# Row sums of the softmax shared by two rows, later turns on TensorE, six probability buffers, and one spread for two maxima, in a hybrid attention layer on one Trainium2 core

## The chip, the cores and the metric

The program runs on one core of one Trainium2 chip. The metric is the device time of one execution in microseconds (us). Three executions of the kernel before took 1028.60, 1028.52 and 1027.94 us, with a median of 1028.52 us. The engines are called as in the profile: PE is TensorE, DVE is VectorE, ACT is ScalarE, POOL is GpSimd, and SP is the engine that issues most of the DMAs.

## What is computed

One encoder layer over 1024 tokens of width 1024. A normed input goes through one projection into the queries, keys and values of two token mixers. Group A is attention in a sliding window with a learned sink logit for each of its 8 heads; group B is neighbourhood attention on a 16 x 64 grid with 8 heads. Their outputs are normed, joined and projected, and a gated feed-forward part follows. The change touches the softmax of both mixers, and the scales of the output projection. Cut to that:

```python
# group A, per block of 128 queries and 384 keys (256 at the ends)
s = einsum('bqgrd,bkgd->bgrqk', q_i, k_i) * scale
s = where(valid, s, -1e30)
m = maximum(max(s, axis=-1), sink_gr)
p = exp(s - m[..., None])
denom = sum(p, axis=-1) + exp(sink_gr - m)
o = einsum('bgrqk,bkgd->bgrqd', p, v_i) / denom
...
# group B
p = softmax(s + bias)
o = einsum('bhcij,bicjhd->bchd', p, v_win)
...
h = h + einsum('bse,ed->bsd', concat([rmsnorm(o_a), rmsnorm(o_b)]), w_out)
```

## The kernel before

All matrix products are made to single-precision accuracy from two halves, a high and a low part: three matmuls for each block of weights. PE runs its instructions in the order in which the program is written. The other engines are ordered by a scheduler, which moves instructions about within their dependences and priorities; each engine then works through its own list strictly in that order.

The attention stage lies between about 60 us and 345 us of the span. It is cut into *units*. Group A has 16 units (2 key heads x 8 blocks of queries), each with four *rows* (one row is one head and one block: 128 queries against 384 or 256 keys). Group B has 32 units, four for each of 8 heads, each with two rows. A unit's work on PE is a list of *events*: a score step for a row (`q_step`, two matmuls at L436), a value step (`v_step`, L525 in group A, L601 in group B) and, for some rows, a *turn* (four lines from L495, the matmuls at L498). Score steps run two to three units ahead of the value steps that use their rows. Between two events `fill` puts in blocks of the projections that are still owed (L172 to L174, three matmuls each), and later of the output projection (L180), by the rates in `RATES`. So PE has something to do nearly always.

A row passes through `softmax` (L458 to L492). On DVE, L466 adds the mask or bias to the scores, writes them to a buffer `p` and finds the row's extreme. On ACT, L470 takes the exponential and sums it into `sm`. On DVE, L471 takes the reciprocal of `sm`, one instruction for each row. Then the row leaves by one of four paths:

- T: POOL scales the row (L474); later PE turns it over by three transposes into a bank `pt` (L498), ACT copies the high part (L501) and DVE the low part (L502).
- D: DVE makes `by`, the reciprocal times a constant (L484); ACT writes the high part to a staging tile (L485), DVE the low part (L487), and a transposing DMA, here called a *flip*, carries both to the tile `turned` (L492, issued by SP).
- P: POOL scales the row (L474), ACT and POOL make the two parts (L480, L481), and a flip follows.
- Q: as D, but the low part is made on POOL by two instructions, a scaled copy `y` (L490) and a subtraction (L491).

Group A's rows go D, P, T, T (`PATH_A`); group B's go Q, Q, T, Q, Q, Q, T, Q for the eight blocks of a head (`PATH_B`). Two rows next to each other share one tile `turned` (the class `Rows`), of which three are in rotation, with a few spare ones. The buffers `p` are five in rotation (`PS`), `y` has one (`YS`); staging tiles are three. In group A, POOL first copies the sink logit into the buffer (L465).

Where turns stand among a unit's events is set by hand: `T_NEXT = (3, 8)` puts the two turns of the next unit at places 3 and 8 of this unit's events while group A is worked on, `T_B` does so in group B, and `T_AT` holds for the first unit.

`out_scales` (L891 to L903) runs once, at about 190 us. It needs the largest value of a vector of gains and of the rows' sums of the output weights, on all partitions; `top` makes each by a reduction on DVE, one transpose on PE (L255), and a second reduction on DVE (L256).

## Time and profile before

| | us |
|---|---|
| median of three executions | 1028.52 |
| the profiled execution, its own time | 1028.71 |
| the span of that execution, first to last instruction | 1026.6 |
| PE busy, of the span | 1009.0 (98%) |
| DVE busy | 875.2 (85%) |
| ACT busy | 675.8 (66%) |
| POOL busy | 214.6 (21%) |

The profiled execution's time is 2.1 us above its span, and 0.2 us above the median. The granted clock of PE is 0.997 of full speed. Matmuls overlap, so what PE's busy time shows is not how close to its peak it is; what it does show are the stretches in which PE stood still, and the view of waits says for whom. A number in brackets behind a row of a timeline is the time that the engine sat idle before that instruction, and who released it.

### The profile page before, as it was taken

The page shows a single profiled execution, that of the slowest core. Times are in us where ns is not written, and L with a number is a line of the kernel's source. Part 1 is how long each engine was busy: PE and PEld are TensorE (multiplying, and loading weights), DVE is VectorE, ACT ScalarE, POOL GpSimd, SP SyncE. Part 2 cuts the span into 40 slices and gives each one's busy share as a digit, 9 for nine tenths or more (in the row PEclk, how much of TensorE's full clock was granted, in tenths as well). Part 3 has the DMA queues.
Part 4 walks back from the last instruction along what each step waited for, and adds up shares of the span by engine and source line. Part 5 has one row for each costly group of instructions (what it writes and reads, how often), then busy time and mean ns, then how long its engine had stood idle before and what let it go on. Part 6 is the DMA issues. An engine that isn't in the chain of part 4 may idle for free.

```text
span 1026.6 us, 15663 instructions
## 1 busy us (share of the span) xinstructions
PE 1009.0 (98%) x5102; PEld 577.2 (56%) x5102; DVE 875.2 (85%) x1715; ACT 675.8 (66%) x1242; POOL 214.6 (21%) x339
## 2 busy tenths in 40 slices
PE   8999999999999999999999999999999999999996
PEld 6877777777775555544444444444444444444446
DVE  6799997767898799999897989888888879999865
ACT  7667787768687687645777777844544656655551
POOL 2225545777976210001000000000000000000002
PEclk9999999999999999999999999999999999999998
DMA  8566564786799874201787777723232778978734
GB/s 318 194 134 134 111 141 102 154 160 134 141 190 226 287 254 165 82 1 42 258 279 248 262 242 250 246 99 128 87 122 89 256 250 306 309 242 269 257 141 164
DMA packets 143938, 191.79 MB, mean 187 GB/s; under 512 B 77360, under 2 KB 88112, under 8 KB 143856
## 3 DMA queue, kind: packets, MB, share of 16 engines
q1 hardware_dynamic: 133264, 164.84, 56.2%
q10 hardware_dynamic: 10592, 25.95, 6.6%
q8 instruction: 40, 0.66, 0.3%
q14 instruction: 42, 0.34, 0.1%
HBM read 132.81 MB, written 28.57 MB: 157 GB/s over the span
## 4 chain that ended last, share of the span: by engine, by line
PE 75%; DVE 3%; DMA 2%; ACT 1%; issue 0%; POOL 0%; DVEq 0%; ACTq 0%; POOLq 0%
PE pj L180 7%; PE dn L1199 6%; PE dn L1198 6%; PE dn L1197 6%; PE z L1197 5%; PE z L1198 5%; PE z L1199 5%; PE x L1197 4%; PE y L1197 4%; PE x L1198 4%; PE y L1198 4%; PE y L1199 4%; PE x L1199 4%; PE pj L172 3%; PE pj L174 2%; PE pj L173 2%
## 5 line engine op out<-in xcount | busy, mean ns | idle before, releaser
L1199 PEld LDWEIGHTS <-wlo 128*128 128x128 f16 x898 | 87.9, 98 | 101.3
L1197 PEld LDWEIGHTS <-whi 128*128 128x128 f16 x898 | 88.1, 98 | 100.3
L1198 PEld LDWEIGHTS <-whi 128*128 128x128 f16 x898 | 87.9, 98 | 100.2
L1199 PE MATMUL dn<-xd,wlo 128*128 128x512 f16 (+1 forms) x330 | 120.4, 365 | 0.0
L1198 PE MATMUL dn<-xd,whi 128*128 128x512 f16 (+1 forms) x330 | 120.4, 365 | 0.0
L1197 PE MATMUL dn<-xd,whi 128*128 128x512 f16 (+1 forms) x330 | 120.4, 365 | 0.0
L172 PE MATMUL pj<-xgh,whi 128*128 128x512 f32 x248 | 106.8, 431 | 0.0
L1197 PE MATMUL z<-hg,whi 128*128 128x512 f16 x264 | 100.1, 379 | 0.0
L1198 PE MATMUL z<-hg,whi 128*128 128x512 f16 x264 | 100.1, 379 | 0.0
L1199 PE MATMUL z<-hg,wlo 128*128 128x512 f16 x264 | 100.1, 379 | 0.0
L470 ACT ACTIVATE p<-p,nm 128x385 f32<-128x385 f32 (+3 forms) x128 | 74.8, 584 | 35.7 <-DVE nm L466 27.1
L174 PE MATMUL pj<-xgh,wlo 128*128 128x512 f32 x248 | 97.7, 394 | 0.0
L173 PE MATMUL pj<-xgl,whi 128*128 128x512 f32 x248 | 97.4, 393 | 0.0
L1171 ACT ACTIVATE whi<-ws,m 128x512 f16<-128x512 f32 (+1 forms) x96 | 65.9, 708 | 35.6 <-DVE ws L1338 20.4
L1172 DVE SCALAR_TENSOR_TENSOR wlo<-ws,m,whi 128x512 f16<-128x512 f32 (+1 forms) x96 | 70.2, 741 | 17.9 <-ACT whi L1171 17.7
L1052 POOL TENSOR_TENSOR back<-back,cst 128x4 f32<-128x4 f32 (+1 forms) x7 | 2.8, 394 | 356.7 <-DVE back L1051 356.7
L1186 ACT ACTIVATE scan<-scan 128x1024 f32<-128x1024 f32 (+1 forms) x60 | 61.1, 1018 | 18.0 <-DMA scan<-in_w_down_dram 13.6
L1171 ACT ACTIVATE whi<-raw,m 128x512 f16<-128x512 f32 (+1 forms) x78 | 51.3, 699 | 17.7 <-DMA raw<-in_w_down_dram 9.6
L1172 DVE SCALAR_TENSOR_TENSOR wlo<-raw,m,whi 128x512 f16<-128x512 f32 (+1 forms) x78 | 55.4, 731 | 6.9 <-ACT whi L1171 6.9
L1197 PE MATMUL y<-hg,whi 128*128 128x512 f16 x160 | 60.6, 379 | 0.0
L1198 PE MATMUL y<-hg,whi 128*128 128x512 f16 x160 | 60.6, 379 | 0.0
L1199 PE MATMUL y<-hg,wlo 128*128 128x512 f16 x160 | 60.6, 379 | 0.0
(299 smaller groups left out, 2457.7 us busy)
## 6 DMA issues: line engine op xcount, KB each, us to landing
xd<-x SPq DMA_DIRECT2D x77, 256.0 KB, 5.5
raw<-in_w_down_dram SPq DMA_DIRECT2D x64, 256.0 KB, 3.6
x<-c ACTq DMA_DIRECT2D x22, 512.0 KB, 3.7
scan<-in_w_gate_dram SPq DMA_DIRECT2D x18, 512.0 KB, 4.5
scan<-in_w_up_dram SPq DMA_DIRECT2D x18, 512.0 KB, 6.1
raw<-in_w_gate_dram SPq DMA_DIRECT2D x18, 512.0 KB, 3.9
raw<-in_w_up_dram SPq DMA_DIRECT2D x18, 512.0 KB, 3.5
raw<-in_w_in_dram SPq DMA_DIRECT2D x32, 256.0 KB, 3.1
```

What stands on the lines that cost most here:

```text
L172: nc.tensor.matmul(ps, w[0], x[0][:, tsl(h)], start=first, stop=False)
L173: nc.tensor.matmul(ps, w[0], x[1][:, tsl(h)], start=False, stop=False)
L174: nc.tensor.matmul(ps, w[1], x[0][:, tsl(h)], start=False, stop=last)
L180: nc.tensor.matmul(ps, a, b, start=i == 0 and b is x[h][0] and a is w[0], stop=i == len(ws) - 1 and a is w[1])
L470: nc.scalar.activation(p[:, 0:e], p[:, 0:e], AF.Exp, bias=nm, scale=-1.0, accum_out=sm)
L1052: nc.gpsimd.tensor_tensor(back, back, unit_back.to_broadcast([128, n]), op=ALU.mult)
L1171: mark["whi"] = nc.scalar.activation(hi, src, AF.Copy, scale=by)
L1172: nc.vector.scalar_tensor_tensor(lo, src, by, hi, op0=ALU.mult, op1=ALU.subtract)
L1186: nc.scalar.activation(t, t, AF.Square, accum_out=dst)
L1197: nc.tensor.matmul(ps, w[0], x[0], start=first and i == 0, stop=False, skip_group_check=True)
L1198: nc.tensor.matmul(ps, w[0], x[1], start=False, stop=False, skip_group_check=True)
L1199: nc.tensor.matmul(ps, w[1], x[0], start=False, stop=last and i == len(ws) - 1, skip_group_check=True)
```

## The change

Four edits.

1. `softmax` no longer takes the reciprocal itself. It keeps the row in a list, and its sum goes to one column of a tile of two. With the second row of a pair it calls the new `share`: one reciprocal over both columns, one product for `by` over the columns of the rows on paths D and Q, and then `leave` for the first row and for the second. `leave` is what followed the reciprocal before.
2. `T_NEXT` goes from (3, 8) to (5, 10).
3. `p` has six buffers instead of five, and `y` no buffer of its own: it takes one of the six.
4. `top` becomes `tops`: two reductions into two columns, two transposes into one bank, and one reduction for both.

```diff
-TURNED, PS, HLS, SPARE_A, LOWS = 3, 5, 1, (2, 5), 1
+TURNED, PS, HLS, SPARE_A, LOWS = 3, 6, 1, (2, 5), 1
...
-T_B, T_NEXT = (0, 3), (3,8)
+T_B, T_NEXT = (0, 3), (5, 10)
...
-        def top(rows, tag, name):
-
-            v, m = (cpool.tile([128, 1], F32, name=name + x, tag=name + x) for x in "vm")
-            nc.vector.tensor_reduce(v, rows, axis=mybir.AxisListType.X, op=ALU.max, apply_absolute_value=True)
+        def tops(groups, tag):
+
+            n = len(groups)
+            v, m = (cpool.tile([128, n], F32, name=x) for x in ("tv", "tm"))
+            for i, rows in enumerate(groups):
+                nc.vector.tensor_reduce(v[:, i:i + 1], rows, axis=mybir.AxisListType.X, op=ALU.max, apply_absolute_value=True)
             ps = bank("wm", tag)
-            nc.tensor.transpose(ps[:, 0:128], v.to_broadcast([128, 128]), ident)
-            nc.vector.tensor_reduce(m, ps[:, 0:128], axis=mybir.AxisListType.X, op=ALU.max)
-            return m
+            for i in range(n):
+                nc.tensor.transpose(ps[:, 128 * i:128 * i + 128], v[:, i:i + 1].to_broadcast([128, 128]), ident)
+            nc.vector.tensor_reduce(m, ps[:, 0:128 * n].rearrange("p (c w) -> p c w", w=128), axis=mybir.AxisListType.X, op=ALU.max)
+            return [m[:, i:i + 1] for i in range(n)]
...
+                self.rows = []
...
-                    nm, sm = (spool.tile([128, 1], F32, name=x) for x in ("nm", "sm"))
+                    nm = spool.tile([128, 1], F32, name="nm")
+                    if not self.rows:
+                        self.sums = spool.tile([128, 2], F32, name="sm")
+                    i = len(self.rows)
+                    sm = self.sums[:, i:i + 1]
...
-                    nc.vector.reciprocal(sm, sm)
-                    x = apart(p[:, 0:n])
+                    self.rows.append((path, j, c, apart(p[:, 0:n]), skip))
+                    if i:
+                        self.share()
+                    return (lambda: self.turn(j, p, c, skip)) if path == "T" else None
+
+            def share(self):
+
+                nc.vector.reciprocal(self.sums, self.sums)
+                whole = [i for i, row in enumerate(self.rows) if row[0] in "DQ"]
+                by = spool.tile([128, 2], F32, name="by") if whole else None
+                if whole:
+                    cols = slice(whole[0], whole[-1] + 1)
+                    nc.vector.tensor_scalar(by[:, cols], self.sums[:, cols], P_TOP, None, op0=ALU.mult)
+                for i, row in enumerate(self.rows):
+                    self.leave(*row, self.sums[:, i:i + 1], by[:, i:i + 1] if i in whole else None)
+
+            def leave(self, path, j, c, x, skip, sm, by):
+
                     if path in "PT":
                         mark["scaled"] = nc.gpsimd.tensor_scalar(x, x, sm, P_TOP, op0=ALU.mult, op1=ALU.mult)
                     if path == "T":
-                        return lambda: self.turn(j, p, c, skip)
+                        return
...
-                        by = spool.tile([128, 1], F32, name="by")
-                        nc.vector.tensor_scalar(by, sm, P_TOP, None, op0=ALU.mult)
...
-                            y = apart(apool.tile([128, 384], F32, name="y", tag="y", bufs=YS)[:, 0:n])
+                            y = apart(apool.tile([128, 384], F32, name="y", tag="p", bufs=PS, padded_shape=[128, 386])[:, 0:128 * c])
...
-            m = top(par[:, C_NA:C_NA + 8], "pt", "og")
+            m, s = tops([par[:, C_NA:C_NA + 8], wo_rows], "pt")
...
-            s = top(wo_rows, "pt", "ow")
```

The number of instructions on PE, ACT and POOL and of DMAs is the same as before. DVE has 81 fewer: 64 reciprocals, 16 products for `by` (group A's 16 stay, group B's 48 become 32) and one reduction of `tops`. Behind the attention stage no engine's list is changed. In the changed kernel the lines are moved: scores L439, mask and extreme L474, reciprocal L486, `by` L491, scaling L498, `y` L512, subtraction L513, flips L514, turns L520, the low part of a turn L524, values of group A L547.

Three places show how instructions move.

PE in group A, in the middle of the stage, at about 141 us of the span: the stretch between two value steps in which the first turn of a pair stood or stands. `s` are scores, `pj` a projection block, `o` values, `pt` the bank of a turn, `turned` the tile of a pair. Before:

```order
L498 MATMUL pt_1846<-cst_89,p_1778 128x128 x3
L172 MATMUL pj_1818<-xgh_201,whi_1359 128x512
L173 MATMUL pj_1818<-xgl_202,whi_1359 128x512
L174 MATMUL pj_1818<-xgh_201,wlo_1360 128x512
L436 MATMUL s_1855<-ka_746,q_813 128x384
L436 MATMUL s_1855<-kb_747,q_813 128x384
L525 LDWEIGHTS v_470
L525 MATMUL o_1822<-turned_1587,v_470 128x256
```

Now:

```order
L439 MATMUL s_1796<-ka_740,q_805 128x384
L439 MATMUL s_1796<-kb_741,q_805 128x384
L172 MATMUL pj_1774<-xgh_201,whi_1327 128x512
L173 MATMUL pj_1774<-xgl_202,whi_1327 128x512
L174 MATMUL pj_1774<-xgh_201,wlo_1328 128x512
L547 LDWEIGHTS v_470
L547 MATMUL o_1778<-turned_1551,v_470 128x256
L547 LDWEIGHTS v_470
L547 MATMUL o_1778<-turned_1551,v_470 128x256
L520 MATMUL pt_1819<-cst_89,p_1736 128x128 x3
```

The first turn of a pair (`p_1778` before, `p_1736` now) stood ahead of a projection block, a score step and a value step; now it stands behind them. DVE at the same place, where `p_1778` and `p_1809` are the two turned rows of the pair before, and `p_1736` and `p_1756` now; an L466 (now L474) finds a row's extreme. Before, from the first row's reciprocal to the second row's:

```order
L471 RECIPROCAL sm_1780<-sm_1780 128x1
L466 ISA p_1809,nm_1810<-s_1806,cst_89,nsink_168 128x384
L466 ISA nm_1810 128x1
L466 ISA p_1829,nm_1830<-s_1826,cst_89,nsink_168 128x384
L466 ISA nm_1830 128x1
L540 TENSOR_TENSOR mixa_1793<-o_1695,ot_1791 64x2x128
L471 RECIPROCAL sm_1811<-sm_1811 128x1
```

Now, from the first row's extreme to the reciprocal for both:

```order
L474 ISA p_1736,nm_1737<-s_1733,cst_89,nsink_168 128x384
L474 ISA nm_1737 128x1
L524 TENSOR_TENSOR turned_1597<-pt_1726,turned_1597 128x3x128
L509 SCALAR_TENSOR_TENSOR stage_628<-p_1662,by_1698,stage_628 128x3x128
L474 ISA p_1756,nm_1757<-s_1753,cst_89,nsink_168 128x384
L474 ISA nm_1757 128x1
L276 TENSOR_TENSOR t_1616<-pj_1617,rstd1_370 128x8x8x8
L524 TENSOR_TENSOR turned_1597<-pt_1767,turned_1597 128x3x128
L486 RECIPROCAL sm_1738<-sm_1738 128x2
```

Before, the first of the two had a reciprocal of its own, and the extreme of the next unit's first row (`p_1829`) stood between; now the one reciprocal stands behind the second row's extreme, an evacuation of a projection (L276) and a low part (L524).

DVE in the first units of group A, at about 75 to 78 us of the span. L342 and L269 are of the projections, `turned_689` before and `turned_685` now are the tile of the first unit's two turned rows, `turned_758` and `turned_752` that of the second unit's. Before:

```order
L342 TENSOR_TENSOR kb_747<-t_503,ka_746 64x1024
L269 TENSOR_TENSOR t_779<-pj_780,rstd1_370 128x512
L502 TENSOR_TENSOR turned_758<-pt_852,turned_758 128x3x128
L471 RECIPROCAL sm_839<-sm_839 128x1
L502 TENSOR_TENSOR turned_689<-pt_863,turned_689 128x2x128
```

Now:

```order
L345 TENSOR_TENSOR kb_741<-t_503,ka_740 64x1024
L272 TENSOR_TENSOR t_771<-pj_772,rstd1_370 128x512
L524 TENSOR_TENSOR turned_685<-pt_840,turned_685 128x2x128
L524 TENSOR_TENSOR turned_752<-pt_848,turned_752 128x3x128
```

The low part of the first unit's second turn (`turned_689`, `turned_685`) stood behind the low part of another unit's turn and behind a reciprocal; now it stands directly behind L269, ahead of the other turn's.

POOL and SP in group B, at about 300 us, at the third pair of a head (two rows on path Q). POOL before, with the first row's `y_3995` and the second row's `y_4021`:

```order
L490 TENSOR_SCALAR y_3995<-p_3986,sm_3988 128x384
L491 TENSOR_TENSOR stage_618<-y_3995,stage_618 128x3x128
L490 TENSOR_SCALAR y_4021<-p_4012,sm_4014 128x384
L491 TENSOR_TENSOR hl_619<-y_4021,hl_619 128x3x128
L474 TENSOR_SCALAR p_4063<-p_4063,sm_4065 128x384
```

Now, with `y_3878` and `y_3883` for the same two rows:

```order
L512 TENSOR_SCALAR y_3878<-p_3852,sm_3854 128x384
L512 TENSOR_SCALAR y_3883<-p_3870,sm_3854 128x384
L513 TENSOR_TENSOR stage_628<-y_3878,stage_628 128x3x128
L513 TENSOR_TENSOR hl_629<-y_3883,hl_629 128x3x128
L498 TENSOR_SCALAR p_3925<-p_3925,sm_3927 128x384
```

Before, each row's subtraction followed its own scaled copy; now both copies come first, and the first row's subtraction third. SP's list there, with `turned_3982` before and `turned_3848` now as the tile of this pair, `xr` and `raw` loads of 512 KB and 256 KB. Before:

```order
L679 DMA xr_4217<-in_xT_dram 128x1024
L492 DMA_TRANSPOSE turned_3982<-stage_618 128x6x128
L150 DMA raw_4329<-in_w_out_dram 128x512
L492 DMA_TRANSPOSE turned_3982<-hl_619 128x6x128
L150 DMA raw_4455<-in_w_out_dram 128x512
```

Now:

```order
L701 DMA xr_4071<-in_xT_dram 128x1024
L150 DMA raw_4179<-in_w_out_dram 128x512
L514 DMA_TRANSPOSE turned_3848<-stage_628 128x6x128
L514 DMA_TRANSPOSE turned_3848<-hl_629 128x6x128
L514 DMA_TRANSPOSE turned_3921<-stage_628 128x4x128
```

The first row's flip stood ahead of a load of `raw`, and now stands behind it, right ahead of the second row's.

More of the change, by code (lines that the diff above doesn't have):

```diff
@@ L37 @@
 AHEAD = 4
-TURNED, PS, HLS, SPARE_A, LOWS = 3, 5, 1, (2, 5), 1
+TURNED, PS, HLS, SPARE_A, LOWS = 3, 6, 1, (2, 5), 1
 LEAD = 3
-BIAS0, YS = 8, 1
+BIAS0 = 8
 T_AT = (0, 4)
 PATH_A, PATH_B = "DPTT", ["QQTQQQTQ"] * 8
-T_B, T_NEXT = (0, 3), (3,8)
+T_B, T_NEXT = (0, 3), (5, 10)
 SPARE_B = [(1, 3), (1, 3), (3,), ()]
```

## Prediction

> **What bounds the kernel now.** I read the page first, for which engine fills the span.
>
> ```profile
> span 1026.6 us, 15663 instructions
> ...
> PE 1009.0 (98%) x5102; PEld 577.2 (56%) x5102; DVE 875.2 (85%) x1715; ACT 675.8 (66%) x1242; POOL 214.6 (21%) x339
> ```
>
> PE is busy for 98% of the span, and the change takes no instruction from PE. So it can only gain what PE spends standing still in the stage that it touches, and it can only lose by making PE stand still longer. Next the busy times by windows over the attention stage; the columns are PE, PE's weight loads, DVE, ACT and POOL, each with its number of instructions, then the granted clock and the DMA share.
>
> ```profile
> 50.00:100.00 50.00, 48.10 (x253) 38.18 (x252) 46.69 (x129) 33.74 (x79) 19.04 (x42) 1.00 0.65 135
> 100.00:150.00 50.00, 49.04 (x285) 37.17 (x284) 46.13 (x146) 40.80 (x107) 26.34 (x57) 1.00 0.62 126
> 150.00:200.00 50.00, 49.35 (x282) 37.75 (x281) 39.86 (x138) 37.01 (x95) 30.61 (x52) 1.00 0.56 117
> 200.00:300.00 100.00, 100.00 (x556) 78.61 (x555) 76.86 (x217) 72.50 (x158) 78.63 (x91) 1.00 0.80 152
> 300.00:350.00 50.00, 48.80 (x294) 29.46 (x293) 39.46 (x113) 35.66 (x79) 26.55 (x38) 1.00 0.95 223
> ```
>
> PE's idle time is 1.90 + 0.96 + 0.65 us in group A (50 to 200), nothing from 200 to 300, and 1.20 us from 300 to 350: 4.71 us in all. That is the ceiling of any gain here, under half a per cent. In group A DVE is busy for 92 to 93% of the first two windows, which makes it the engine that comes nearest to holding PE up. Third, PE's waits say for whom those 4.71 us were.
>
> ```profile
> PE o L525 <- DVE by L484: 1.4, 1, 1.4
> PE pt L498 <- POOL p L474: 1.4, 3, 0.7
> ...
> PE o L601 <- DMA turned<-hl: 0.6, 1, 0.6
> ...
> PE o L601 <- DMA turned<-stage: 0.5, 1, 0.5
> ...
> PE pt L498 <- DVE turned L502: 0.3, 1, 0.3
> PE wm L255 <- DVE nm L466: 0.2, 1, 0.2
> ```
>
> The columns are total, times, longest. There are eight waits worth naming: one for the low part of a turn at the first unit, three turns that wait for POOL's scaling, one that waits for a bank, two for flips in group B, and one in the spread of the maxima. (The first row names `by`, but see below.)
>
> **The change part by part.** *DVE's small instructions.* The reciprocals and products that go, by their groups:
>
> ```profile
> L471 DVE RECIPROCAL sm<-sm 128x1 f32<-128x1 f32 x128 | 19.8, 156 | 19.7 <-ACT p L470 19.0
> L484 DVE TENSOR_SCALAR by<-sm 128x1 f32<-128x1 f32 x64 | 9.5, 149 | 1.2
> ```
>
> 64 x 0.156 + 16 x 0.149 us = 12.4 us of DVE's busy time go. I expect a column more to cost nothing that can be seen, since these instructions work on one element a partition. None of the 12.4 us is on the path: PE's waits show DVE as its bound for 1.9 us in all, and 19.0 us of its idle time was spent waiting for ACT's sums in front of a reciprocal anyway. So the term itself is 0; it counts through the waits that follow. [...]
>
> *The first unit's wait, 1.4 us.* PE and, around it, DVE:
>
> ```profile
> 77.69 0.27 PE L525 MATMUL o<-turned,v 128*128 128x256 f16 x1 [1.42 <-DVE by L484]
> ```
>
> ```profile
> 76.11 0.68 DVE L269 TENSOR_TENSOR t<-pj,rstd 128x512 f32<-128x512 f32 x1
> 76.71 0.54 DVE L502 TENSOR_TENSOR turned<-pt,turned 128x384 f16<-128x384 f32 x1
> 77.18 0.14 DVE L471 RECIPROCAL sm<-sm 128x1 f32<-128x1 f32 x1
> 77.25 0.39 DVE L502 TENSOR_TENSOR turned<-pt,turned 128x256 f16<-128x256 f32 x1
> ```
>
> What PE needs is the low part that ends at 77.25 + 0.39 = 77.64. In the new order it stands directly behind L269 and would start at 76.71, 0.54 us sooner. I take -0.5. The bounds are 0, if ACT's high part comes no sooner, and -1.4.
>
> *The later turns, three waits of 1.4 us.* The longest, 0.70 us, with what PE does behind it, and DVE's work on the two rows of that pair:
>
> ```profile
> 141.40 0.55 PE L498 MATMUL pt<-cst,p 128*128 128x128 f32 x3 [0.70 <-POOL p L474]
> 142.48 0.33 PE L436 MATMUL s<-ka,q 128*128 128x384 f32 x1
> ...
> 143.76 0.33 PE L436 MATMUL s<-ka,q 128*128 128x384 f32 x1
> ```
>
> ```profile
> 137.50 0.61 DVE L466 CUSTOM_DVE_ANT_0 p<-s,cst,nsink 128x384 f32<-128x384 f32 x1
> ...
> 138.81 0.56 DVE L502 TENSOR_TENSOR turned<-pt,turned 128x384 f16<-128x384 f32 x1
> 139.28 0.68 DVE L273 TENSOR_TENSOR t<-pj,rstd 128x512 f32<-128x512 f32 x1
> 139.88 0.15 DVE L471 RECIPROCAL sm<-sm 128x1 f32<-128x1 f32 x1
> 139.95 0.60 DVE L466 CUSTOM_DVE_ANT_0 p<-s,cst,nsink 128x384 f32<-128x384 f32 x1
> ...
> 141.59 0.16 DVE L471 RECIPROCAL sm<-sm 128x1 f32<-128x1 f32 x1
> ```
>
> ```profile
> L474 POOL TENSOR_SCALAR p<-p,sm 128x384 f32<-128x384 f32 x52 | 35.0, 674 | 35.3 <-DVE sm L471 35.1
> ```
>
> Two things work against each other. The turn moves behind a projection block, a score step and a value step, which is what lies between the scores at 142.48 and 143.76: 1.28 us. Without its wait it would have begun at 140.70, so PE now comes to it at 141.98. But its row is scaled only after the reciprocal that it shares with the second row. In the trace the first row's extreme is at 137.50 with its reciprocal at 139.88; the second row's are at 139.95 and 141.59. If the shared reciprocal came at 141.59, scaling (0.16 + 0.67, and some 0.1 for the signal) would end at 142.5 and PE would still wait 0.5 us. But in DVE's new list only one low part of a turn (now L524) and one low part on path D (now L509) stand between the two rows' extremes, 0.5 us each as the low part at 138.81 shows, so the second row's can begin at about 137.50 + 0.6 + 1.0 = 139.1; its reciprocal follows 1.64 us behind as it did (139.95 to 141.59), at 140.7, and scaling ends at 141.6, ahead of 141.98. So each of the three waits ends between 0 and 0.5 us; I take nearer to 0, since the new list of DVE is known: -1.2 of the 1.4. The wait for the bank (0.3) goes too, because the turn before it has had its low part read out when PE comes 1.28 us later: -0.3, or 0 if that read-out moves with it. The second turn of a pair also moves by two events; its row's sum comes no later than it did.
>
> *One spread for two maxima.* Both transposes write one bank, so PE has one wait for a bank in place of two: -0.2, with 0 as the other end.
>
> *Flips in group B.* Here the change costs. SP, PE, DVE and POOL at the third pair of a head:
>
> ```profile
> 300.56 0.57 SPq L679 DMA_DIRECT2D xr<-in_xT_dram  x1
> 301.50 1.21 SPq L492 DMA_TRANSPOSE turned<-stage  x1
> 302.80 0.55 SPq L150 DMA_DIRECT2D raw<-in_w_out_dram  x1
> 303.70 1.21 SPq L492 DMA_TRANSPOSE turned<-hl  x1
> ```
>
> ```profile
> 306.10 0.49 PE L601 MATMUL o<-turned,v 128*128 128x256 f16 x4
> ...
> 309.01 0.38 PE L601 MATMUL o<-turned,v 128*128 128x256 f16 x2 [0.65 <-DMA turned<-hl]
> ```
>
> ```profile
> 300.62 0.14 DVE L471 RECIPROCAL sm<-sm 128x1 f32<-128x1 f32 x1
> ```
>
> ```profile
> 300.01 1.46 POOL L491 TENSOR_TENSOR stage<-y,stage 128x384 f16<-128x384 f32 x1
> 301.57 0.59 POOL L490 TENSOR_SCALAR y<-p,sm 128x384 f32<-128x384 f32 x1
> 302.65 1.02 POOL L491 TENSOR_TENSOR hl<-y,hl 128x384 f16<-128x384 f32 x1 [0.50 <-POOL y L490]
> ```
>
> The first row's subtraction ended at 301.47 and its flip went out at 301.50; the second's at 303.67 and 303.70. With a shared reciprocal at 300.62, POOL makes two copies (0.59 each) from about 300.9, then two subtractions (1.02 each): the first ends at about 303.1, 1.7 us later, the second at 304.2, 0.5 us later. The second flip was waited for until 309.01, 5.3 us after its issue. The first flip's tile was read at 306.10 without a wait, so its way took at most 4.6 us; issued at 303.2 it lands by 307.8 at the latest. So PE stands between 0 and 1.7 us at 306.10, and the wait at 309.01 grows by 0.5 or is used up by that standing. I take +0.9, the middle, because this window has the DMA engines 95% busy, and because a load of 256 KB now goes out ahead of the first flip. The next head has such a pair with no wait today; +0.1 for it, between 0 and 1. What is queued behind the later flip on SP are these same loads, which nobody has waited for in this window. The wait of 0.5 us for `turned<-stage` belongs to a pair with a turned first row; its flip row is the second, and POOL makes it as before: 0.
>
> *Six buffers.* The extra buffer lets POOL's copy of a sink start one row sooner; as `y` now takes turns in the same six, a `y` can have to wait for a turned row's transposes. In PE's list those turns come first, which is the cover, so 0; if it fails, POOL stops until the turn, about one event, 1.3 us, and everything behind it on POOL with it.
>
> The sum: -0.5 - 1.2 - 0.3 - 0.2 + 0.9 + 0.1 = -1.2 us. The profiled execution took 1028.71 us, 0.2 above the median of 1028.5; -1.2 from the median gives **1027.3 us**. A measurement of this kernel can tell about 0.2% from no change, 2.1 us, and this gain is less than that.
>
> **The rivals.** *All of group A's idle time goes, and group B hides its flips:* DVE has 80 small instructions less, most of them where it was over 90% busy or in front of its long ones, so that the low parts come early everywhere. Then 1.90 + 0.96 + 0.65 us go, 3.5 us, and the time is 1025.0. For it speaks that each named wait of group A ends on DVE or on what DVE releases; against it the window from 300, where DMA is the engine waited for. Chance 0.36.
>
> *The shared sum holds POOL and the flips up: slower.* The first flip of each Q, Q pair is up to 1.7 us later. There are two such pairs in a head, and eight in the last four heads, where the DMA share rises from 0.80 to 0.95. It decides from the point at which a first flip lands behind its first L601: then each pair costs what it is late. At 0.9 us each, eight pairs cost 7.2 us, less group A's 2.2: +5.0, 1033.5 us. For it speaks that two flips are waited for already; against it that from 200 to 300 PE had no idle time at all, so that flips there had room. Chance 0.13. [...]
>
> *The gain is not there:* DVE's freed time only lengthens its waits for ACT (the 19.0 us), the turns wait as long at their new places, and group B costs its 1.0: 1029.5, or 1028.5 without that. Chance 0.14.
>
> **How the numbers follow.** My forecast, a gain of less than 2.1 us, has 0.37. With the last rival it makes no measurable change: 0.51. Faster is 0.36, slower 0.13. The low end is the sum with its best bounds: -1.4 - 1.4 - 0.3 - 0.2 = -3.3, and some of the rest of group A's idle time, 1024.8. The high end takes no gain and the flips' worst, +1.7 and a little at the next head, 1030.4; the slower rival beyond it is left out.
>
> **What would show it.** In the changed kernel's waits of PE, the rows of L498 on POOL and on DVE (now L520) should be gone or under 0.3 us in all, and the first unit's wait should be under 1.0. PE's idle time from 50 to 200 should be about 1.4 us. There should be 64 reciprocals. From 300 to 350 the waits on flips (L601, now L623) should sum to 1.5 to 3 us. The forecast is wrong if PE shows idle time from 200 to 300, if a turn waits at every unit, or if the stage behind the attention differs, since no list of instructions changes there.

## The result, and the profile after

The changed kernel took 1036.59 us (median of six executions, 1033.91 to 1038.25), beside 1028.34 us for the kernel before. The ratio is 1.0077, with an interval of 1.0066 to 1.0089: by it the change costs 7.9 us (the two medians lie 8.2 us apart). The profiled execution has a span of 1034.5 us, 7.9 us more than before.

The line of the page on the engines:

```profile
PE 1012.1 (98%) x5102; PEld 578.4 (56%) x5102; DVE 873.0 (84%) x1634; ACT 674.3 (65%) x1242; POOL 209.7 (20%) x339
```

DVE has 81 instructions less, as planned, and the other engines have as many as before. The busy times by windows, with the same columns as before, show the place:

```profile
50.00:100.00 50.00, 49.12 (x260) 39.14 (x258) 46.63 (x122) 34.95 (x83) 19.73 (x43) 1.00 0.61 138
100.00:150.00 50.00, 49.62 (x290) 37.81 (x289) 44.31 (x128) 39.60 (x105) 25.71 (x57) 1.00 0.60 124
150.00:200.00 50.00, 48.83 (x277) 37.05 (x275) 39.70 (x122) 36.59 (x96) 30.99 (x51) 1.00 0.61 124
200.00:300.00 100.00, 99.01 (x549) 77.47 (x548) 76.41 (x188) 71.88 (x158) 73.33 (x89) 1.00 0.67 146
300.00:350.00 50.00, 43.16 (x244) 25.47 (x243) 32.72 (x85) 30.98 (x71) 25.54 (x38) 0.93 0.71 173
```

Group A did gain: PE's idle time there is 0.88 + 0.38 + 1.17 = 2.43 us in place of 3.51. But from 200 to 300 there is 0.99 us where there was none, and from 300 to 350 there are 6.84 us in place of 1.20, with a granted clock of 0.93 in place of 1.00. PE's waits name the operations:

```profile
PE o L623 <- DMA turned<-stage: 4.8, 1, 4.8
PE pt L520 <- POOL p L498: 4.3, 5, 2.1
...
PE o L547 <- DVE turned L524: 0.5, 1, 0.5
PE s L439 <- DVE nm L474: 0.4, 1, 0.4
```

The first unit's wait fell from 1.4 to 0.5 us (L547), and the turn's wait for a bank and the wait in the spread of the maxima are gone; a score step at 154.74 now waits 0.4 us (L439). New are one wait of 4.8 us for a flip, and turns that wait for POOL for 4.3 us in place of 1.4. Where these lie, in PE's timeline:

```profile
82.15 0.55 PE L520 MATMUL pt<-cst,p 128*128 128x128 f32 x3 [0.43 <-POOL p L498]
...
104.96 0.55 PE L520 MATMUL pt<-cst,p 128*128 128x128 f32 x3 [0.38 <-POOL p L498]
...
296.83 0.55 PE L520 MATMUL pt<-cst,p 128*128 128x128 f32 x3 [0.99 <-POOL p L498]
...
302.66 0.27 PE L623 MATMUL o<-turned,v 128*128 128x128 f16 x2
307.70 0.40 PE L623 MATMUL o<-turned,v 128*128 128x256 f16 x2 [4.77 <-DMA turned<-stage]
...
330.87 0.55 PE L520 MATMUL pt<-cst,p 128*128 128x128 f32 x3 [2.07 <-POOL p L498]
```

The fifth turn that waits, 0.41 us, stands at 198.44. The large ones all lie in group B, at pairs whose first row is turned (T) and whose second is flipped (Q). In the kernel before, PE read the same flip without a wait:

```profile
302.98 0.65 PE L601 MATMUL o<-turned,v 128*128 128x128 f16 x4
```

How the pair at 297 came about is read on DVE first. Its T row's extreme stands at 288.63, its Q row's at 292.84, and the shared reciprocal at 295.05:

```profile
288.63 0.55 DVE L474 CUSTOM_DVE_ANT_0 p<-s,xb 128x384 f32<-128x384 f32 x1
...
290.33 2.59 DVE L201 TENSOR_TENSOR mg<-mixa,mg 128x1024 f16<-128x1024 f32 x2 [1.14 <-ACT mg L200]
292.84 0.55 DVE L474 CUSTOM_DVE_ANT_0 p<-s,xb 128x384 f32<-128x384 f32 x1
...
295.05 0.15 DVE L486 RECIPROCAL sm<-sm 128x2 f32<-128x2 f32 x1
```

Two splits of the mixers' output (L201) stand between the two rows. Before, the T row did not depend on the second one; now POOL sits idle for 4.60 us until the second row's sum, and all that stands behind the T row's scaling on POOL comes late. In POOL's list these are the copy `y`, the two instructions that make the next head's bias table (L581, L582), and then the subtraction that the flip waits for. On SP, the load of the next raw bias (`rr`) had to wait for those tables, and it and a load of x go out directly ahead of the flip. The kernel before, POOL and then SP:

```profile
293.41 0.59 POOL L474 TENSOR_SCALAR p<-p,sm 128x384 f32<-128x384 f32 x1 [2.46 <-DVE sm L471]
...
294.92 1.71 POOL L560 TENSOR_TENSOR xb<-cst,rr 128x256 f32<-128x256 f32 x1
...
298.31 0.93 POOL L491 TENSOR_TENSOR stage<-y,stage 128x384 f16<-128x384 f32 x1
```

```profile
296.65 0.61 SPq L548 DMA_DIRECT2D rr<-in_rpb_dram  x1
297.31 0.58 SPq L679 DMA_DIRECT2D xr<-in_xT_dram  x1
299.26 1.24 SPq L492 DMA_TRANSPOSE turned<-stage  x1
```

The changed kernel, POOL and then SP:

```profile
295.30 1.48 POOL L498 TENSOR_SCALAR p<-p,sm 128x384 f32<-128x384 f32 x1 [4.60 <-DVE sm L486]
296.75 0.58 POOL L512 TENSOR_SCALAR y<-p,sm 128x384 f32<-128x384 f32 x1
...
298.25 1.17 POOL L582 TENSOR_TENSOR xb<-cst,rr 128x256 f32<-128x256 f32 x1
299.39 0.92 POOL L513 TENSOR_TENSOR stage<-y,stage 128x384 f16<-128x384 f32 x1
```

```profile
299.45 0.61 SPq L570 DMA_DIRECT2D rr<-in_rpb_dram  x1
300.11 0.58 SPq L701 DMA_DIRECT2D xr<-in_xT_dram  x1
300.79 1.25 SPq L514 DMA_TRANSPOSE turned<-stage  x1
```

The joint sum holds the scaling for 1.9 us (POOL waited 2.46 us there before, too). The subtraction comes 1.1 us later than before and the flip 1.5 us, but both loads 2.8 us: they went out 2.6 and 2.0 us ahead of the flip, and now 1.3 and 0.7 us. PE had its product ready to go at 302.9 and got the flip at 307.7, 6.9 us after its issue. Last, the granted clock (the number ahead of the DMA share) in short windows around the two long waits:

```profile
302.00:307.00 5.00, 0.93 (x7) 0.46 (x6) 1.59 (x5) 1.25 (x5) 2.63 (x4) 1.00 1.05 168
307.00:309.00 2.00, 1.30 (x6) 0.73 (x5) 0.09 (x1) 1.24 (x3) 0.60 (x1) 0.73 1.05 389
309.00:312.00 3.00, 3.00 (x11) 1.41 (x11) 3.00 (x6) 2.62 (x6) 0.07 (x1) 0.61 0.97 212
...
331.00:333.00 2.00, 2.00 (x12) 1.45 (x12) 1.12 (x6) 1.89 (x7) 1.65 (x4) 0.70 0.62 240
333.00:336.00 3.00, 3.00 (x13) 1.52 (x12) 2.73 (x5) 2.08 (x4) 1.84 (x3) 0.63 0.27 49
```

Each long wait is followed by a stretch at a lower clock: 2 x 0.27 + 3 x 0.39 = 1.7 us lost behind the first, 2 x 0.30 + 3 x 0.37 = 1.7 us behind the second. So from 300 to 350 us PE lost 4.77 + 2.07 + 3.4 = 10.2 us where it lost 1.2 before. With the 0.99 at 297 and group A's gain of 1.08 that makes +8.9 us; the span grew by 7.9. The last 1.0 us, spread over the other stages, isn't followed here.

### The profile page after: what moved, and what is told of

The parts are those of the page before. It is cut to its first block, busy times and chain, and to the rows that moved or that the text cites. A ratio compares the mean times of both kernels' runs of the same rounds, so it can differ in the third digit from the quotient of the medians.

```text
span 1034.5 us, 15469 instructions
## 1 busy us (share of the span) xinstructions
PE 1012.1 (98%) x5102; PEld 578.4 (56%) x5102; DVE 873.0 (84%) x1634; ACT 674.3 (65%) x1242; POOL 209.7 (20%) x339
## 4 chain that ended last, share of the span: by engine, by line
PE 62%; DVE 2%; DMA 1%; ACT 0%; issue 0%; SPq 0%; POOL 0%; DVEq 0%; ACTq 0%
PE dn L1218 6%; PE dn L1219 6%; PE dn L1220 6%; PE z L1218 5%; PE z L1220 5%; PE z L1219 5%; PE pj L180 4%; PE y L1218 4%; PE y L1220 4%; PE y L1219 4%; PE x L1218 4%; PE x L1220 4%; PE x L1219 4%; PE ss L1258 1%; DMA rw<-in_w_gate_dram 1%; DVE mixb L1163 0%
```

## The experiments

*Theory:* the joint sum in group B ties a turned row to its partner; that makes one flip late, and the late flip makes most of the rest. *Rivals:* the six shared buffers hold POOL up; the later turns do; three staging tiles are too few; or it is luck in the order of the DMAs. A pair of group B is called T, Q or Q, Q by the paths of its rows. Times and ratios (with intervals) of all runs, each against the kernel before on the same chip (1028.1 to 1028.7 us there):

| run | us | ratio |
|---|---|---|
| pairs in group A only | 1028.77 | 0.9999 (0.9991 to 1.0008) |
| no pairs, rest of the change | 1028.30 | 0.9993 (0.9984 to 1.0002) |
| pairs, without the rest | 1044.34 | 1.0152 (1.0138 to 1.0166) |
| T, Q pairs let go | 1030.05 | 1.0013 (1.0004 to 1.0022) |
| Q, Q pairs let go | 1034.46 | 1.0066 (1.0052 to 1.0080) |
| turns of group B two events later | 1037.26 | 1.0083 (1.0068 to 1.0098) |
| tables free | 1030.46 | 1.0019 (1.0009 to 1.0028) |
| tables free from head 2 on | 1030.01 | 1.0016 (1.0008 to 1.0025) |
| fourth staging tile, five buffers | 1036.32 | 1.0076 (1.0063 to 1.0089) |
| raw bias load behind the flip | 1029.97 | 1.0016 (1.0007 to 1.0025) |
| pairs in A, own buffer for y | 1028.35 | 1.0002 (0.9991 to 1.0013) |
| pairs in A, fourth staging tile | 1027.82 | 0.9990 (0.9980 to 0.9999) |
| the same, tables free | 1029.21 | 1.0006 (0.9997 to 1.0015) |
| the same, turns one event later | 1031.60 | 1.0030 (1.0019 to 1.0041) |
| the same, raw load behind the flip | 1027.75 | 0.9995 (0.9986 to 1.0004) |

In the experiments' kernels, line numbers are up to 7 higher, and 3 lower in that of the pairs alone. Where an expectation speaks of PE's *standing*, it is summed from the starts of the matmuls and comes out 0.8 to 2.8 us above the idle time of the windows.

**Which part of the change costs.** The first edit lets `Rows` be told whether it shares, and a row that doesn't share leaves at once:

```diff
+PAIRED = lambda group, paths: group == "A"
-                    if i:
+                    if i or not self.paired:
                         self.share()
```

> Pairs keep their joint sum in group A alone; each row of group B leaves by a reciprocal of its own, as in the kernel before. Everything else of the change stays (later turns, six shared buffers, joint spread). Theory (the joint sum in group B holds the turned row and POOL's list until the second row, 8.9 us of PE's standing between 300 and 350 us and 1.2 at 297): those 10 us go and group A's gain of about 1.1 us stays, so 1026 to 1028.5 us, and no wait of PE over 1.5 us in group B. Rival (y in the six shared buffers holds POOL up in group B): the 4.8 us wait stays, 1034 to 1038. Rival (it is luck of the DMA order, set off by any change of the list): somewhere between, with a wait at another flip.

Its windows from 200 us on:

```profile
200.00:300.00 100.00, 100.00 (x556) 78.39 (x555) 78.24 (x213) 71.51 (x156) 78.06 (x89) 1.00 0.82 154
300.00:350.00 50.00, 47.52 (x286) 28.15 (x285) 39.41 (x111) 36.20 (x80) 26.96 (x38) 1.00 0.89 209
```

The loss is gone, with six shared buffers in place: it is the pairs of group B. Group A keeps its gain (2.16 us of idle time from 50 to 200 us, where the kernel before had 3.51), but PE's idle time from 300 to 350 is 2.48 us, where the kernel before had 1.20, so that the sum comes out at no change, 0.3 us above what was expected.

With the same edit and `PAIRED` false everywhere:

> No pairs at all: every row has a reciprocal and a product of its own; later turns, six shared buffers and joint spread stay. Theory (joint sums in group B): within 1 us of the kernel with pairs in group A alone, 1026.5 to 1029, group A losing or winning what the joint sums there are worth (bounds 0 and 1.2 us, from group A's idle time of 2.4 against 3.5 us). Rival (shared buffers): 1034 to 1038.

1028.30 us: without any joint sum the kernel is as fast as with one in group A. The joint sum itself brings nothing that can be measured. The opposite, the pairs alone with `T_NEXT = (3, 8)`, `PS = 5`, `y` in a buffer of its own and two spreads:

> The joint sum alone, in both groups; turns as early as before, five buffers and y in one of its own, two spreads as before. Theory (joint sums in group B): slower by the same 9 to 10 us from 290 to 350 us, and group A loses too, since turns that come 1.3 us sooner wait for a joint sum: 1036 to 1042. Rival (shared buffers): 1027 to 1031.

It is slower still, by 1.5%. The first line of its waits of PE:

```profile
PE pt L517 <- POOL p L495: 13.2, 12, 2.3
```

Twelve turns, in both groups, wait for POOL's scaling; nine of them, 9.9 us, come before 190 us, where the changed kernel has two waits of 0.8 us in all. This run takes back three things at once, but these waits are those that the later turns are meant to end. So the later turns look less like a gain beside the pairs than like what the pairs need. The time lies above the expected range, since I had not reckoned with a dozen of them.

Then pairs by their paths, `PAIRED = lambda group, paths: paths != "TQ"`:

> Only the pairs of group B whose first row is turned (T, Q) are let go: each of their rows has a reciprocal of its own; the Q, Q pairs of group B and all of group A keep the joint sum. Theory in its narrow form (it is the T, Q pair: its turned row waits for the second row, POOL idles 4.6 us and everything behind it comes late): the waits at 297, 308 and 331 us go, 1026.5 to 1029. In its wide form (any pair of group B): part of it stays, as late first flips of Q, Q pairs, 1029.5 to 1034. Rival (shared buffers): 1034 to 1038.

and the counterpart, `paths == "TQ" or group == "A"`:

> The counterpart of the experiment that let the T, Q pairs of group B go (1030.05 us): here they alone keep the joint sum in group B, and the Q, Q pairs' rows leave singly; group A keeps pairs. Theory (the T, Q pairs carry nearly all of the loss): the waits at 297, 308 and 331 us are all there, 1034.5 to 1037. Rival (it takes late Q, Q pairs ahead of it for the T, Q pair to be late): the wait at 308 goes below 2 us, 1029 to 1033.

Letting the T, Q pairs go leaves +0.13%; keeping them alone leaves +0.66%. Together that is about the 0.77%. The T, Q pairs carry nearly all of it, and they need no late Q, Q pair ahead of them: the run that keeps them has its long wait at the same place,

```profile
PE o L627 <- DMA turned<-stage: 6.0, 2, 5.0
```

while the other has one of 2.1 us there, for a flip that SP issued at 300.86 with the raw load 2.2 us ahead of it. This is still the Q row of a T, Q pair, and no longer tied to its partner: it was late because the first of the two table instructions took 3.59 us on POOL, where it takes 0.98 in the changed kernel. Why it did is not shown.

**Why a flip that is 1.5 us late costs 5 us.** The kernel before issued this flip at 299.26, the changed one at 300.79. First, the turns' own part: `T_B = (2, 5)` in place of `(0, 3)`.

> The whole change, but a turn of group B stands two events later in PE's list (about 2.6 us by the scores of group A that the prediction quoted, 1.28 us apart for one event). Theory (a turned row of a T, Q pair is scaled only after the second row's sum, and so are the flips behind it): the turns' own waits of 0.99 and 2.07 us at 297 and 331 us go with the slow rows behind the second, about 5 us, 1031 to 1033; the flip's wait of 4.8 us at 308 stays unless the low part that now comes later moves it, as POOL still gets the pair's sum late. Rival (the flip is late only because PE's turn was late and moved what follows): the 4.8 us go too, 1026 to 1029. Rival (later turns hold their rows' buffers longer, and the six are short): POOL stands for a buffer, 1036 or more.

```profile
PE o L623 <- DVE turned L524: 4.8, 6, 1.1
PE o L623 <- DMA turned<-hl: 2.3, 2, 1.6
PE o L623 <- DMA turned<-stage: 2.1, 1, 2.1
```

My numbers failed here. The turns' waits went, but six waits for the turned rows' low parts came in their place, and with the flips' 4.4 us the time is much the same, 1037.26 us. Waiting later did not help, and this run does not say what made the long wait of 4.77 us. Next, the bias tables, which by the scheduler's rule stand behind the last scaling of a turned row:

```diff
-            with behind(*["scaled"] * (h > 0)):
+            if True:
```

> The whole change, but the two instructions that make a head's bias table no longer have to stand behind the last scaling of a turned row on POOL, so that none stands between a copy and its subtraction in the list at the second pair of heads 5 and 6. Theory (the pair's late sum, 4.6 us of idle POOL, is most of the lateness of the flip that PE waited 4.8 us for; the tables, 0.98 + 1.17 us, are the rest): the flip goes out about 1.2 to 2.1 us sooner and the wait falls from 4.8 to 1.5 to 3.6 us; the turns' waits stay: 1032 to 1035. Rival (the tables are the whole cause, and the flip's long way of 6.8 us comes of meeting the loads): the wait goes below 0.5 us, 1029 to 1031.

```diff
-            with behind(*["scaled"] * (h > 0)):
+            with behind(*["scaled"] * (h == 1)):
```

> The whole change, but the bias tables of heads 2 to 7 no longer have to stand behind the last scaling of a turned row (that of head 1 still has to, which the earlier experiment without this changed as well, with a wait of 1.6 us at 59 us). Theory (late sum and tables together make the one flip late; each alone is hidden): as in that experiment no flip is waited for over 1 us and the turns' waits stay at about 1 us each; without the wait at 59 us 1.3 us less than its 1030.5: 1028.5 to 1030.5. Rival (that experiment's gain was luck with the DMA order): a wait of 2 us or more for a flip is back, 1032 or more.

Both bring the ratio from 1.0077 down to 1.0019 and 1.0016, with the joint sums all in place. The second one's waits, and POOL and SP at the pair:

```profile
PE pt L520 <- POOL p L498: 3.7, 5, 1.2
...
PE o L623 <- DMA turned<-hl: 0.7, 1, 0.7
```

```profile
296.32 1.48 POOL L498 TENSOR_SCALAR p<-p,sm 128x384 f32<-128x384 f32 x1 [4.60 <-DVE sm L486]
...
298.45 0.92 POOL L513 TENSOR_TENSOR stage<-y,stage 128x384 f16<-128x384 f32 x1
```

POOL idles the same 4.60 us for the joint sum, and PE doesn't mind. So the late sum alone is not enough, nor are the tables alone (the kernel before has them there too). My bet had been that the tables are the smaller half; the rival's "below 0.5 us, 1029 to 1031" was right. A fourth staging tile (`PS = 5, HLS = 2`) tests another rival:

> The whole change with pairs in both groups, but five buffers that rows and copies share and a fourth staging tile in the place of the sixth. Theory (the pair's late sum, with the bias table ahead of the subtraction, makes the flip late at its issue): the wait of PE of 4.8 us at 308 keeps 3 us or more, and the turns' waits of 1 and 2 us stay; ACT no longer stands 4.5 us for a staging tile there, so that what follows comes sooner: 1032 to 1036. Rival (it was the scarcity of staging tiles that made the flip late or held it): the wait goes below 1 us, 1028 to 1031.

The wait keeps its 4.8 us, and the time is 1036.32, a little more than expected: too few staging tiles are not the cause. That left two ways in which tables could matter: their 2.15 us on POOL, or the raw load behind them on SP. The next kernel leaves POOL's list alone and changes SP's only:

```diff
-            nc.sync.dma_start(raw, src)
+            with behind(*[("flip", h - 2)] * (h > 1)):
+                nc.sync.dma_start(raw, src)
...
+                    if b == 3:
+                        mark["flip", h] = mark["flip"]
```

> The whole change with POOL's list as it is; only a head's raw bias load (rr, 128 rows of 1956 bytes) has to stand behind one more flip in SP's list, that of the second pair two heads earlier. In the changed kernel SP waits with that load until the tables are made, 299.45 us, and sends it and a load of x (300.11) directly ahead of the flip of 300.79 that landed 6.8 us later. Theory A (the late tables matter because SP sends their next raw load ahead of the flip): the flip goes out about 300.35, its way is 4 us or less, PE's wait of 4.8 us falls below 1.5, and the time is 1029.5 to 1032.5 us, with the turns' waits of 1 and 2 us still there. Theory B (the tables matter by their 2.15 us on POOL ahead of the subtraction): the wait falls by the 0.45 us of the earlier issue and little more, to 3 us or over, 1034 to 1036.

POOL, SP and PE at the pair:

```profile
298.33 1.18 POOL L583 TENSOR_TENSOR xb<-cst,rr 128x256 f32<-128x256 f32 x1
299.47 0.92 POOL L513 TENSOR_TENSOR stage<-y,stage 128x384 f16<-128x384 f32 x1
```

```profile
295.36 0.73 SPq L704 DMA_DIRECT2D xr<-in_xT_dram  x1
300.42 1.23 SPq L514 DMA_TRANSPOSE turned<-stage  x1
301.70 1.38 SPq L704 DMA_DIRECT2D xr<-in_xT_dram  x1
303.13 0.62 SPq L571 DMA_DIRECT2D rr<-in_rpb_dram  x1
```

```profile
304.39 0.38 PE L626 MATMUL o<-turned,v 128*128 128x256 f16 x2 [1.38 <-DMA turned<-stage]
```

The tables and the subtraction stand as late on POOL as in the changed kernel (0.08 us apart), and still PE's wait is 1.38 us in place of 4.77, and the ratio falls from 1.0077 to 1.0016. The load of x now goes out at 295.36, since SP no longer stands in front of it waiting for the tables. The flip's way is 4.0 us in place of 6.9. The turn's wait of 2.07 us at 331 and both stretches at a lower clock went with it (no turn waits for over 1.0 us in this run, and the clock from 300 to 350 us is 1.00); they followed from the first wait. So theory A of the expectation holds: the late tables matter by what SP sends behind them. Three different edits, at the pair, at the tables and at the load, each cut the chain at another link, and each brings the kernel to 1030.0 to 1030.5 us. That makes luck in the order of the DMAs unlikely as the explanation, though not impossible. The trace of the changed kernel shows how long the raw load was under way. The view of the tile `rr` has for its eight loads there

```profile
DMA to landing us min/median/max: 5.0/5.3/5.5
```

so the load sent at 299.45 was under way until 304.4 at least; the flip sent 1.34 us behind it reached PE after that, at 307.70. As the load of x moved too, this run doesn't tell how much of the 2.9 us is due to either load. Nor do the runs below, where both go out ahead of it; they show how the flip's way goes with the time that the two have ahead of it:

| run | raw load and load of x, us ahead of the flip | flip issued, reached PE | way, us |
|---|---|---|---|
| changed kernel | 1.34, 0.68 | 300.79, 307.70 | 6.9 |
| fourth staging tile, five buffers | 1.34, 0.67 | 301.49, 308.41 | 6.9 |
| T, Q pairs let go | 2.21, 1.55 | 300.86, 305.13 | 4.3 |
| kernel before | 2.61, 1.95 | 299.26, by 302.98 | at most 3.7 |

So it is the two loads directly ahead of the flip that are left for the 2.9 us, though the other transfers around differ too. The joint sum makes flips late, but not always at such a cost: with the pairs alone PE waits for two of the flips from `stage`, for 1.9 and 0.5 us.

**Looking for a version that beats both.** Pairs in group A alone, with `y` in a buffer of its own again; or with five shared buffers and a fourth staging tile:

> Pairs in group A alone, as in the first experiment, but with five buffers for rows and the copy y in one of its own again. In that experiment group A kept 1.5 us of gain (its standing 4.7 in place of 6.3 us) and the stretch from 300 to 350 us lost 1.7 (3.7 in place of 2.0), with every row of group B leaving as before. Theory (six shared buffers move group B's copies and flips): 300 to 350 us falls back to 1.5 to 2.5, and the time is 1026 to 1028 us, if group A doesn't need the sixth buffer. Rival (the stretch from 300 on depends on when group A ends, whatever the buffers): 3 us or more there, 1028 to 1030.

> Pairs in group A alone, with five buffers that rows and copies share and a fourth staging tile in the place of the sixth. Theory (ACT's high part waits for a staging tile until an earlier flip has landed, and this is what hands one late flip on to the next): the waits for flips from 300 to 350 us shrink from 2.2 us to under 1, 1026 to 1028 us. Rival (the flips' way itself, beside the loads, is what PE waits for): the waits stay at 2 us or more; if five buffers are short for rows and copies, waits for POOL's scaling grow as well, 1029 to 1033.

The first changes nothing (1.0002; PE's idle time from 300 to 350 us is 1.84 us, between the 2.48 with shared buffers and the 1.20 of the kernel before). The second is the fastest, 0.9990 with an interval that ends at 0.9999, half of the 0.2% that a measurement can tell; its waits for flips fell to 1.5 us and not below 1 as expected, so its mechanism isn't shown. Three edits on top of it:

> A version meant to beat both: pairs in group A alone, five shared buffers, four staging tiles (1027.8 us before this edit), and the tables of heads 2 to 7 free of the order behind the scaling. Theory (tables between a copy and its subtraction cost flips from 300 us on even without pairs): the waits there, 3.5 us of standing, fall to 1.5 to 2.5, 1025.5 to 1027.5. Rival (without pairs the scaling is early and the tables are in nobody's way): 1027 to 1029.

> The same version with the tables as they were, but turns of group B one event later. Theory (turns two events later brought 4.8 us of waits for the turns' low part; one event later keeps the low part in time and takes the two turn waits of 0.36 and 0.53 us): 1026.5 to 1028. Rival (the low part's wait begins with the first event): six or more waits for it in group B, 1029 to 1033.

> The best version so far (pairs in group A alone, five shared buffers, four staging tiles; 1027.8 us, ratio 0.999) with the raw bias load behind the flip as well. Theory A of the first kernel of this call: flips from 300 us on wait less (3.5 us of standing there so far, to 2.5 or less), 1026 to 1027.8. Rival (without pairs in group B the load is early enough to be in no flip's way): 1027.5 to 1028.5.

None of them helps: 1.0006, 1.0030 and 0.9995. With the tables free a turn waits 2.2 us for POOL, and with later turns two low parts are waited for, 0.9 us, and flips for longer. So no version beats the kernel before by more than can be measured. A sixth buffer beside a `y` of its own, and a second buffer for the raw bias, weren't tried.

## Why the prediction was wrong, point by point

- *DVE's small instructions, 0:* right. DVE has 81 instructions less, a column more costs next to nothing (the reciprocals of 128x2 take 0.165 us in the median, those of 128x1 before took 0.157), and no pairs at all is as fast as pairs in group A.
- *The first unit's wait, -0.5:* right in kind, more in size (1.42 to 0.45 us).
- *The later turns, -1.2:* mis-sized. The three waits of 1.4 us went, but two others of 0.43 and 0.38 us came in group A, at 82.15 and 104.96, so 0.6 us was gained. The prediction had the two effects, a later turn and a later sum, but took the lower bound of what is left. It also read the wait at 141.40 as the reciprocal's. In the trace of the kernel before, that reciprocal was done at 140.03; POOL was making another row's low part (L481) from 139.87 to 140.79, and scaled this row only then.
- *The bank and the maxima, -0.3 and -0.2:* right, both waits are gone; the new wait of 0.4 us at 154.74 was not foreseen. Group A gained 1.1 us in all, where the sum had 2.2.
- *Flips of group B, +1.0:* this is the step that failed, and with it the forecast. I costed the first flip of Q, Q pairs, and said of a T, Q pair: "its flip row is the second, and POOL makes it as before: 0". On POOL, "as before" does not hold. The T row's scaling stands ahead of the flip row's work in POOL's list, and now waits for the second row's sum; the tables stand behind the scaling, the raw load behind the tables, and the flip behind the raw load and a load of x. I followed POOL's own two instructions for the row and not what stands ahead of them in its list and in SP's. The runs showed in place of the 0 a subtraction 1.1 us later, a flip 1.5 us later with 6.9 us of way, and a wait of 4.77 us with 1.7 us of lower clock behind it; with the T, Q pairs alone keeping the joint sum in group B, the kernel is 0.66% slower than before. With the T, Q pairs let go, 1.3 us are left (1030.05 us, beside 1028.77 with no pairs in group B), near to my +1.0. That is luck: the one long wait there, 2.13 us, is for a T, Q pair's flip, not for the first flip of a Q, Q pair that I costed.
- *Turns of group B:* not costed at all. The prediction spoke of turns only where `T_NEXT` moves them. In group B turns stay where they were, while their rows' sum comes later; that gave 0.99 us at 297, the idle time between 200 and 300 us that was named as what would prove the forecast wrong, and 2.07 us at 331, behind the late flip.
- *Six buffers, 0:* right. With the buffers and without pairs in group B there is no loss.
- *The slower rival* had the cause (the shared sum holds POOL and the flips up) and, at 1033.5 us, the sign. Its place was wrong: not many Q, Q pairs at 0.9 us each, but one T, Q pair whose flip met two loads. The argument set against it, that PE had no idle time from 200 to 300 and flips had room there, failed because a row that nobody waits for has room only up to its partner's sum. The two reciprocals joined saved nothing (1028.30 us with no pairs at all, 1028.77 with pairs in group A) and cost the T row of the pair at 297 its early start: it was scaled 1.9 us later.

## What to carry to other kernels

An instruction shared by two rows makes the earlier row wait for the later one; before joining, look up for each kind of pair how far apart its two inputs come (4.2 us here, where two long splits stand between them), and price that for everything behind the earlier row in each engine's list, not for the two rows alone. On a queue of DMAs, look not only at how late a transfer is issued but also at what goes out directly ahead of it: here two loads that had to wait, released just ahead of a flip, cost 2.9 us on top of the delay (6.9 us of way against 4.0). To find such a link, move one load in one queue and leave the other lists as they are.

## What the runs showed of the hardware

- In the changed kernel two waits of PE were paid twice. Behind the waits of 4.77 and 2.07 us the granted clock was 0.61 to 0.73 in windows of 5 us together, 1.7 us lost each time. In windows of 0.1 us each of these stretches is 3.4 us at a clock of 0.50, from 307.9 and from 331.8 us on. Two other runs have a wait of about 2 us with a lower clock: with the T, Q pairs let go, one of 2.13 us ends at 305.13, and the clock from 300 to 350 us is 0.97; with the pairs alone, one of 2.09 us ends at 92.86, the clock from 50 to 100 us is 0.97, and the three matmuls of a projection block start 0.58 and 0.42 us apart at 93.17, 0.31 and 0.23 at 97.31. So a wait of 2 us can be enough. It need not be: in the version with the fourth staging tile and the tables free, PE's longest wait was 2.2 us; it stood still for 2.24 us between 304 and 307, and the clock there and behind it stayed at 1.00:

```profile
PE pt L524 <- POOL p L502: 3.0, 4, 2.2
```

```profile
304.00:307.00 3.00, 0.76 (x6) 0.32 (x4) 3.00 (x6) 2.74 (x6) 3.00 (x5) 1.00 0.98 169
307.00:309.00 2.00, 2.00 (x15) 1.25 (x13) 1.68 (x5) 1.36 (x4) 1.92 (x3) 1.00 0.47 145
309.00:312.00 3.00, 3.00 (x22) 1.89 (x19) 3.00 (x9) 2.75 (x6) 2.83 (x4) 1.00 0.64 132
```

  What decides between the two is not shown.
- A transposing DMA's way from its issue to PE isn't a fixed time: 4.0 us with SP's last load sent 5.1 us ahead of it (the raw load behind the flip), 4.3 us with a raw load (128 rows of 1956 bytes) and a load of x sent 2.2 and 1.6 us ahead (T, Q pairs let go), 6.9 us with the two sent 1.3 and 0.7 us ahead (changed kernel).
